# One position's row on TensorE in column groups, single-row products padded to whole blocks, the small products of a Fourier layer placed between its projection blocks

## The chip, the cores and the metric

The kernel runs on one core of a Trainium2 chip. The time is the device time of one execution in microseconds (us), the median of three runs. TensorE (PE, with its weight loads PEld), VectorE (DVE), ScalarE (ACT), GpSimd (POOL) and the queue that issues the DMAs (SP) each work through a list of instructions in order, and semaphores join the lists.

## The reference

One inference step of a two-layer backbone, over 1024 latent positions and 256 context positions of 1024 channels in float32. Layer 0 is attention. Layer 1, where the change lies, mixes by a Fourier transform:

```python
def fourier_mix(u):                      # C_GROUPS = 4, C_GROUP_DIM = 256
    b, s, _ = u.shape
    ug = u.astype(jnp.float32).reshape(b, s, C_GROUPS, C_GROUP_DIM)
    f = jnp.fft.fft2(ug, axes=(1, 3), norm="ortho")
    return jnp.real(f).reshape(b, s, C_WIDTH).astype(u.dtype)

def odd_mix(h, w_in, w_out):
    u, gate = jnp.split(h @ w_in, 2, axis=-1)
    return (fourier_mix(u) * jax.nn.silu(gate)) @ w_out
```

`h` is the normalised and modulated input; the result is scaled, added to the residual and normalised once more. Latent and context positions are transformed apart. The output is y of both, and the keys and values of layer 0.

## The kernel before, in words

Products that need more than one pass of precision are made from three: every operand is split into a high part, rounded to the format that TensorE takes in one pass (fp32r), and the low rest; `mm3` (L244 on, its matmul L250) adds high·high, high·low and low·high in a PSUM bank. A split is a copy on ACT (L262 with ACT, L264 with DVE) and a subtraction on DVE or POOL (L268). SBUF is a set of zones of equal buffers (`u`, `w`, `q`, `pt`, `p`, `h`, `e`); `take` and `drop` hand them round, so a tile is named after its zone. PSUM has eight banks: three `s`, one `a`, one `g`, handed out in turn by `next_bank`, and three `t` for transposes. The Python code is not the order of the instructions: a scheduler with a simulated clock sorts them onto the engines.

The Fourier layer's stages, in the order of the code from L1449 on:

- **The one position.** The transform along the positions uses its symmetry: positions are folded into sums and differences, `EH["E"]`, `EH["O"]` and, for the context, `EH["C"]`. One latent position (column 256 of `O`) and one context position (column 128 of `C`) have no partner. Their rows of the projection are computed by themselves. `xo` holds these two columns of the input. `u_load` (L1473) fetches the weights of a projection step (`load_w`, L274) and calls `row` on each raw weight tile: 128 x 2 x 258, two of eight chunks of the contraction. `row` (L1481, L1483) multiplies each chunk by its `xo` scalar per partition on DVE and adds it up in `xacc`: 8 chunks x 2 positions x 2 weight halves = 32 DVE instructions of 128x258. At the start of step n = 2 `xacc` is split, and eight matmuls with a column of ones (`ux`, L1542) add it up over the partitions. The result stands in one partition, `xrow`, and its split in `xrh`, two tiles of one row.
- **The projection blocks.** Four steps n (cosine weights for n = 0, 1; sine weights for n = 2, 3), five position tiles i each. A block is 24 matmuls of 128x258 (n = 0, 1) or 128x256, into a bank named `u` of `next_bank`. Then ACT copies the bank's halves to the high part (L1581), DVE subtracts for the low part (L1582) and, for n = 0 and 1, copies out the columns at frequency 128, `nyr` (L1584). A bank is free when all of these have read it. The blocks of n = 0 and 1 read `E` and, for i = 4, `C`, the others `O` and `C`.
- **The tables.** Cosine and sine tables (`cosl`, `sinl`, `ctab`) are loaded and split while n = 2 and 3 run (`table`, L1491 on); `oddr` is one row that the one position's row is multiplied with.
- **The small products**, after the last block: `pn` and `pn2` (L1609, L1627), the cosine sum of the columns at frequency 128: 21 matmuls with 4 output rows, three pairs of them with one row of contraction only (the position's row times `oddr`); `p5` (L1631), 16 matmuls with two output rows, and `pcol` (L1654), which turns their result into a column. DVE multiplies by the gates and writes to memory (`nyd`).
- **The transform along the positions**: `pcc` for the context, then per channel group g a bank `pc` and a bank `ps` (all L1609). `pcc` has one pair of single-row matmuls per group, `pc` two. DVE and POOL combine the banks and multiply by the gates (L1669 to L1715).
- **The output projection** `of` (L250 by way of `out_proj`), ten tiles of positions with two banks of 24 matmuls of 128x512.

## Time and profile before

| | us |
|---|---|
| median of three runs | 1232.87 (1231.98 to 1237.57) |
| the profiled execution, its own time | 1240.12 |
| its span on the core | 1238.3 |
| busy in the span: PE / PEld / DVE | 1177.0 / 1048.1 / 868.8 |
| busy in the span: ACT / POOL | 580.4 / 313.9 |
| mean granted TensorE clock | 0.976 |

How the views are read: a row of the timeline has the start of the first instruction, the time from that start to the end of the last of the group, engine, line, operation, result <- operands, `rows*columns` of the weights that a matmul uses, the output's shape, and the count. A matmul lasts some 0.28 us by itself but is pipelined, so what one costs is the step from one start to the next. A row of the stages has the stretch, its length, the busy time of the five engines with the instructions in brackets, the granted TensorE clock (1.00 is full speed), the mean share of the DMA engines and GB/s. In a row of the waits the time comes first after the pair, then how often, then the longest. The order of the instructions has no times in it.

### The profile page before, as it was taken

To read this page: it belongs to the slowest core of one execution; us is meant where nothing else is said; L and a number is where in the kernel's file an instruction comes from. 1 tells how busy PE (TensorE), PEld (TensorE's weight loads), DVE (VectorE), ACT (ScalarE), POOL (GpSimd) and SP (SyncE) were. 2 spreads that over 40 slices of the span, in tenths; PEclk is the share of its full clock that TensorE was granted. 3 is DMA by queue.
4 is the path that set the end of the run, shared out by engine and by line. 5 is a ranking of instruction groups with operands and counts; after the bars stand their busy time and mean duration, and the time that the engine had idled before them with its cause. 6 is when DMAs were issued, how large, how long until landed. Compare 5 with 4: busy or idle time off the path is not lost.

```text
span 1238.3 us, 21899 instructions
## 1 busy us (share of the span) xinstructions
PE 1177.0 (95%) x8039; PEld 1048.1 (85%) x8039; DVE 868.8 (70%) x2023; ACT 580.4 (47%) x1163; POOL 313.9 (25%) x270
## 2 busy tenths in 40 slices
PE   6889999999999999999999989889999998999997
PEld 5778889999999998999999877667778888988886
DVE  4378888877676776678878766667766887558553
ACT  3342456555565555556656766422363234332221
POOL 2264543513221230011000033111312225334001
PEclk9999999999999999999999999979999998979999
DMA  9957312323414252344242695777115434254321
GB/s 334 344 171 264 86 58 75 92 82 109 137 60 125 65 155 67 100 111 129 76 135 84 170 266 169 193 220 215 53 43 161 142 116 127 95 187 154 129 91 63
DMA packets 148686, 168.81 MB, mean 136 GB/s; under 512 B 19753, under 2 KB 107605, under 8 KB 148578
## 3 DMA queue, kind: packets, MB, share of 16 engines
q1 hardware_dynamic: 148578, 167.41, 44.3%
q8 instruction: 63, 1.03, 0.3%
q14 instruction: 45, 0.37, 0.1%
HBM read 123.19 MB, written 44.18 MB: 135 GB/s over the span
## 4 chain that ended last, share of the span: by engine, by line
PE 71%; DMA 13%; DVE 8%; ACT 3%; issue 2%; SPq 1%; POOL 1%; POOLq 0%; DVEq 0%; ACTq 0%
PE of L250 9%; PE ga L250 8%; PE av L1012 7%; PE pt L1006 7%; PE q L250 6%; PE oz L250 6%; PE sL L889 4%; PE g1E L250 4%; PE u L250 3%; PE g1O L250 3%; PE kv L250 2%; PE sC L889 2%; DMA h<-i_w_out 2%; DMA q<-qd 2%; DMA u<-i_x 1%
## 5 line engine op out<-in xcount | busy, mean ns | idle before, releaser
L1009 DVE TENSOR_TENSOR pt<-pt,pt 128x512 fp32r<-128x512 f32 (+1 forms) x264 | 171.2, 658 | 44.8 <-ACT pt L262 44.0
L262 ACT ACTIVATE pt<-pt 128x512 fp32r<-128x512 f32 (+1 forms) x264 | 146.6, 576 | 93.3 <-PE pt L1006 60.7
L1012 PE MATMUL av<-pt,u 128*128 128x256 f32 x1008 | 171.1, 291 | 2.1 <-DVE e L1024 1.0
L1006 PE MATMUL pt<-identr,p 128*128 128x128 f32 x1008 | 155.7, 273 | 3.0 <-ACT e L987 2.5
L1012 PEld LDWEIGHTS av<-pt,u 128*128 128x128 f32 x1008 | 141.5, 191 | 7.9 <-DVE e L1024 2.1
L250 PE MATMUL q<-w,u 128*128 128x256 f32 x864 | 133.0, 289 | 1.5 <-DVE u L426 1.2
L1006 PEld LDWEIGHTS pt<-identr,p 128*128 128x128 f32 x1008 | 119.2, 141 | 9.6 <-ACT e L987 2.7
L250 PE MATMUL ga<-u,w 128*128 128x512 f32 (+1 forms) x576 | 124.2, 359 | 0.0
L250 PEld LDWEIGHTS q<-w,u 128*128 128x128 f32 x864 | 116.2, 191 | 6.4 <-DVE u L426 1.5
L930 ACT ACTIVATE p<-p,nm 128x1280 f32<-128x1280 f32 (+1 forms) x80 | 95.3, 1191 | 55.7 <-DVE p L923 52.5
L250 PEld LDWEIGHTS ga<-u,w 128*128 128x128 f32 x576 | 93.6, 188 | 13.5
L268 POOL TENSOR_TENSOR w<-h,w 128x512 fp32r<-128x512 f32 x42 | 56.7, 1369 | 124.6 <-DVE w L264 88.1
L889 PE MATMUL sL<-u,q 128*128 128x512 f32 x256 | 82.3, 413 | 4.8 <-DMA q<-qd 4.8
L930 ACT ACTIVATE p<-p,NM 128x640 f32<-128x640 f32 (+2 forms) x80 | 59.1, 739 | 25.1 <-DVE p L923 24.8
L268 POOL TENSOR_TENSOR u<-h,u 128x512 fp32r<-128x512 f32 x19 | 25.8, 1359 | 173.6 <-ACT u L262 161.0
L889 PE MATMUL sC<-u,q 128*128 128x256 f32 x320 | 64.9, 303 | 0.6 <-DMA q<-qd 0.6
L250 PE MATMUL oz<-u,u 128*128 128x512 f32 x240 | 62.8, 396 | 2.0 <-ACT h L262 1.1
L923 DVE TENSOR_SCALAR_CACHE_REDUCE p<-sL 128x512 f32<-128x512 f32 x64 | 43.8, 684 | 26.2 <-PE sL L889 13.2
L665 POOL TENSOR_TENSOR h<-h,rope 128x512 f32<-128x512 f32 (+1 forms) x18 | 21.6, 1202 | 139.5 <-ACT h L748 100.1
L250 PE MATMUL kv<-w,u 128*128 128x256 f32 x384 | 55.8, 287 | 0.0
L250 PEld LDWEIGHTS oz<-u,u 128*128 128x128 f32 x240 | 44.5, 188 | 12.9 <-ACT h L262 1.3
L889 PEld LDWEIGHTS sC<-u,q 128*128 128x128 f32 x320 | 50.0, 193 | 4.1 <-issue 0.8
(777 smaller groups left out, 2648.9 us busy)
## 6 DMA issues: line engine op xcount, KB each, us to landing
q<-qd SPq DMA_DIRECT2D x80, 256.0 KB
p<-i_ada_w SPq DMA_DIRECT2D x21, 512.0 KB
h<-i_w_in SPq DMA_DIRECT2D x40, 256.0 KB
h<-i_w_out SPq DMA_DIRECT2D x32, 256.0 KB
pt<-i_ada_w SPq DMA_DIRECT2D x14, 512.0 KB
qd<-q SPq DMA_DIRECT2D x22, 256.0 KB
w<-i_wuT SPq DMA_DIRECT2D x8, 512.0 KB
u<-i_x SPq DMA_DIRECT2D x8, 512.0 KB
```

Source lines behind the costliest of these rows:

```text
L250: pe.matmul(out, a, b, start=i == 0, stop=i == n - 1)
L262: act.activation(out, in_, AF.Copy)
L268: pick("lo" + lc, lc).tensor_sub(dst_l, src, dst_h)
L665: pick("rope", XE["rope"]).tensor_mul(t1.rearrange("p t h (b c) -> p t (h b) c", b=2), y.rearrange("p t h (b c) -> p t (h b) c", b=2), cb)
L889: pe.matmul(ps, q_at(q, s, hc), keys, start=s == 0, stop=s == 1)
L923: dve.tensor_scalar(p[i][:, end[i] : end[i] + n], ps, sign, last[i], op0=ALU.mult, op1=ALU.min, accum_out=c)
L930: act.activation(p[i][:, 0 : end[i]], p[i][:, 0 : end[i]], AF.Exp, bias=last[i], scale=-1.0, accum_out=SU[:, t, hd + i, 0:1],)
L1006: pe.transpose(tp[:, jj * 256 + i * P : jj * 256 + i * P + P], p[i][:, off : off + P], ident)
L1009: dve.tensor_sub(pt[:, 1, 0:n], tp[:, 0:n], pt[:, 0, 0:n])
L1012: pe.matmul(acc, vv, pt[:, s, jj * 256 : jj * 256 + 256], start=c + jj + s == 0, stop=c + jj == nt - 1 and s == 1,)
```

## The change

1. `row` no longer runs on DVE. `xo` is widened to 32 columns per chunk, of which two are not zero, and is the weights of four matmuls per raw tile, each 128 rows deep, with 130 columns moving, into 32 output partitions of a `t` bank `xr0` or `xr1`: two chunks x two halves, so the four stand side by side in the columns of the array. They are plain float32, which the program issues as two passes each. One ACT copy per weight half takes the bank out (`xsum`), and eight small float32 matmuls with a selection matrix (`selx`) add the two chunks up into two partitions (`ux`, `ux2`).
2. `xrh` and `oddr` become tiles of 128 rows of which two are not zero (POOL fills them with zeros first). So the single-row matmuls in `pn`, `pn2`, `pcc` and `pc` run over 128 rows.
3. `pn`, `pn2` and `pcol` are placed after the blocks i = 0, 1 and 2 of n = 3 (`AT_F`), in `t` banks. `p5` is gone: `pcol` now takes sixteen matmuls with the blocks of y as weights and the two columns of `alt` moving.

```diff
+AT_F = (0, 1, 2)
...
-    xo = cp.tile([P, 8, 2], F32, name="xo")
+    xo = take("e", (P, 8, 32))
+    pool.memset(xo.a, 0.0)
...
-    xacc = take(("u", "w", "p"), (P, 2, 516))
+    selx = cp.tile([P, 2, 2], F32, name="selx")
+    iv = ident.rearrange("p (a h c) -> p a h c", a=2, h=2)
+    dve.tensor_add(selx, iv[:, 0, :, 0:2], iv[:, 1, :, 0:2])
+    xsum = [take(("u", "w", "p"), (P, 130)) for _ in range(2)]
...
-    xrh = [take(("u", "w", "p"), (1, 2, 516), F32R) for _ in range(2)]
+    xrh = [take(("u", "w", "p"), (P, 516), F32R) for _ in range(2)]
...
     def u_load(n):
         c, hf = divmod(n, 2)
+        ps = t_bank(f"xr{hf}") if c == 0 else None
+
         def row(raw, k0):
-            for v in range(2):
-                acc = xacc[:, v, hf * 258 : hf * 258 + 258]
-                for k in (k0, k0 + 1):
-                    x = raw[:, k - k0, :]
-                    if k == 0:
-                        dve.tensor_scalar(acc, x, xo[:, k, v : v + 1], None, op0=ALU.mult)
-                    else:
-                        dve.scalar_tensor_tensor(
-                            out=acc, in0=x, scalar=xo[:, k, v : v + 1], in1=acc, op0=ALU.mult, op1=ALU.add
-                        )
+            for kk in range(2):
+                for h in range(2):
+                    j = 2 * kk + h
+                    pe.matmul(
+                        ps[32 * j : 32 * j + 32, 0:130], xo[:, k0 + kk, :], raw[:, kk, 128 * h : 128 * h + 130],
+                        start=k0 == 0, stop=k0 == 6,
+                    )
+            if k0 == 6:
+                act.activation(xsum[hf].a, ps[:, 0:130], AF.Copy)
...
+    def fine_part(i):
+        if i == 0:
+            fine["a"] = t_bank("pn")
+            cos_pair(fine["a"][0:4, :], ny, xn(0))
+        elif i == 1:
+            fine["b"] = t_bank("pn2")
+            cos_sum(fine["b"][0:4, 0:256], [ny(4)], [ctcol(0)], xn(1), oddr[:, 512:768])
...
+        elif i == 2:
+            pcol = t_bank("pcol")
+            for g in range(4):
+                for n in range(4):
+                    pe.matmul(pcol[:, 2 * g : 2 * g + 2], y_at(0, n // 2, g)[n % 2], alt, start=n == 0, stop=n == 3)
+            dve.tensor_scalar(p5c, pcol[:, 0:8:2], scale, None, op0=ALU.mult)
...
-            xh, xl = [take(("u", "w", "p"), (P, 2, 516), F32R) for _ in range(2)]
-            act.activation(xh.a, xacc.a, AF.Copy)
-            dve.tensor_sub(xl.a, xacc.a, xh.a)
...
-                    ps = next_bank(f"ux{h2}{v}")[0:2, 0:258]
-                    for m, x in enumerate((xh, xl)):
-                        pe.matmul(ps, ones2[:, 0, :], x[:, v, sl], start=m == 0, stop=m == 1)
...
+                    out = ps[0:2, (2 * h2 + h) * P : (2 * h2 + h) * P + P]
+                    pe.matmul(out, selx[:, h, :], xsum[h2][:, h : h + P], start=True, stop=True)
...
+            for x in xrh:
+                pool.memset(x.a.bitcast(F32), 0.0)
...
-            oddr, oraw = take(BIG, (1, 768), F32R), take(BIG, (1, 768))
+            oddr, oraw = take(BIG, (P, 768), F32R), take(BIG, (2, 768))
+            pool.memset(oddr.a.bitcast(F32), 0.0)
...
+            if n == 3 and i in AT_F:
+                fine_part(AT_F.index(i))
...
-    cos_pair(pn[0:4, :], ny, xn(0))
...
-            pe.matmul(p5[0:2, g * P : g * P + P], alt, y_at(0, n // 2, g)[n % 2], start=n == 0, stop=n == 3)
```

What the scheduler makes of it is shown at three places, as the rows of the order stand, before and after. **DVE, where the first projection blocks are taken out of PSUM.** L1483 and L1481 are the position's row, L1582 and L1584 (after: L1674 and L1676) the evacuation of a bank `u`, L1394 (L1395) a gate. Before:

```order
L1483 SCALAR_TENSOR_TENSOR p_12065<-w_12110,xo,p_12065 128x258 x2
L1483 SCALAR_TENSOR_TENSOR p_12065<-p_12118,xo,p_12065 128x258 x4
L1483 SCALAR_TENSOR_TENSOR p_12065<-pt_12128,xo,p_12065 128x258 x2
L1582 TENSOR_TENSOR u_12169<-u_12176,u_12169 128x128
L1483 SCALAR_TENSOR_TENSOR p_12065<-pt_12128,xo,p_12065 128x258 x2
L1582 TENSOR_TENSOR u_12169<-u_12206,u_12169 128x128
L1483 SCALAR_TENSOR_TENSOR p_12065<-q_12136,xo,p_12065 128x258
L1582 TENSOR_TENSOR u_12172<-u_12176,u_12172 128x128
L1584 COPY nyr<-u_12176 128x2
```

After:

```order
L1434 TENSOR_TENSOR h_12021<-g1c_11994,h_12019 128x128
L1395 SCALAR_TENSOR_TENSOR h_12021<-u_12024,h_12021 128x256
L1674 TENSOR_TENSOR u_12177<-u_12184,u_12177 128x128
L1674 TENSOR_TENSOR u_12180<-u_12184,u_12180 128x128
L1676 COPY nyr<-u_12184 128x2
L1674 TENSOR_TENSOR u_12177<-u_12214,u_12177 128x128
```

The evacuation of the first bank now follows the last gate directly.

**PE, at the start of the projection.** `ad12p` is a small sum of another row, `xr` the new matmuls in column groups. Before:

```order
L353 MATMUL ad12p_12029<-h_12036,ones_88 2x512
L250 MATMUL u_12176<-w_12072,w_10787 128x258
L250 MATMUL u_12176<-p_12073,w_10787 128x258
L250 MATMUL u_12176<-w_12072,w_10788 128x258
L250 MATMUL u_12176<-w_12072,p_10811 128x258
```

After:

```order
L354 MATMUL ad12p_12029<-h_12036,ones_88 2x512
L1487 MATMUL xr_12076<-pt_12079,e_12058 32x130 x4
L1487 MATMUL xr_12076<-q_12087,e_12058 32x130
L354 MATMUL ad12p_12029<-h_12037,ones_88 2x512
L1487 MATMUL xr_12076<-pt_12097,e_12058 32x130 x4
L251 MATMUL u_12184<-p_12077,w_10787 128x258
L251 MATMUL u_12184<-u_12078,w_10787 128x258
L1487 MATMUL xr_12076<-w_12105,e_12058 32x130 x4
L251 MATMUL u_12184<-p_12077,w_10788 128x258
```

The 32 matmuls of `xr` stand in six sets, of 5, 7, 4, 4, 4 and 8, within and between the first blocks; a set reads the raw weight tile straight from its DMA.

**SP, around the loads of the tables.** `i_cosl` is the cosine table, `i_w_out` weights of the output projection into buffers `h`, `g1d` gates. Before:

```order
L1068 DMA h_12939<-i_w_out 128x512
L1068 DMA h_12925<-i_w_out 128x512
L1567 DMA h_12706<-g1d 4x256
L1564 DMA p_12703<-g1d 128x4x256
L1498 DMA u_12690<-i_sinl 128x1024
L1498 DMA u_12531<-i_cosl 128x1024
```

After:

```order
L1069 DMA h_12942<-i_w_out 128x512
L1069 DMA h_12922<-i_w_out 128x512
L1069 DMA h_12926<-i_w_out 128x512
L1069 DMA h_12932<-i_w_out 128x512
L1069 DMA h_12936<-i_w_out 128x512
L1505 DMA u_12695<-i_sinl 128x1024
L1647 DMA w_12700<-i_oddr 2x768
L1656 DMA u_12707<-g1d 128x4x256
L1656 DMA w_12709<-g1d 128x4x256
L1505 DMA u_12536<-i_cosl 128x1024
```

Five loads of output weights instead of two now stand ahead of the tables, and both gate loads ahead of the cosine table, which `pn` reads after sixteen blocks instead of twenty. The last four of the five use buffers `h` that held the raw sine weights of n = 3.

## The prediction

> **What bounds the kernel now.** I read the page first, then the stages of the Fourier layer, then PE's timeline inside them. TensorE is busy almost throughout, so a gain must come from PE's own time:

> ```profile
> PE 1177.0 (95%) x8039; PEld 1048.1 (85%) x8039; DVE 868.8 (70%) x2023; ACT 580.4 (47%) x1163; POOL 313.9 (25%) x270
> ```

> The stages tell where that time is poor. Columns: stretch, length, busy PE, PEld, DVE, ACT, POOL, granted TensorE clock, DMA share, GB/s.

> ```profile
> 1033.30:1037.40 4.10, 0.14 (x2) 0.07 (x1) 4.10 (x13) 2.27 (x6) 1.52 (x4) 0.88 0.47 126
> 1036.00:1037.00 1.00, 0.00 (x0) 0.00 (x0) 1.00 (x3) 0.74 (x3) 0.31 (x2) 0.71 0.03 8
> 1043.00:1044.00 1.00, 1.00 (x9) 1.00 (x8) 0.17 (x2) 0.00 (x0) 1.00 (x2) 0.88 0.61 205
> 1094.00:1095.00 1.00, 1.00 (x6) 0.64 (x5) 0.96 (x2) 0.00 (x0) 0.93 (x1) 0.72 0.50 174
> 1108.00:1109.00 1.00, 1.00 (x10) 1.00 (x10) 0.87 (x2) 0.09 (x1) 0.00 (x0) 0.95 0.12 49
> ```

> PE stands still from 1033.3 to 1037.4 while DVE is busy for all of it. The clock is 1.00 or 0.50: a mean of 0.71 in 1036 to 1037 puts the fall at 1036.42, 0.88 puts the return at 1043.24, and in the same way the second stretch at half speed runs from 1094.44 to 1108.10. These stretches are 6.82 and 13.66 us long, and the falls lie 58.02 apart: 2, 4 and 17 times 3.41, as if the clock were set anew every 3.41 us on a grid of its own. What ended the standstill, and DVE's work there:

> ```profile
> 1037.36 1.63 PE L250 MATMUL u<-u,w 128*128 128x258 f32 x6 [3.96 <-DVE nyr L1584]
> L1483 DVE SCALAR_TENSOR_TENSOR p<-w,xo,p 128x258 f32<-128x258 f32 x6 | 5.8, 999 | 0.0
> L1481 DVE TENSOR_SCALAR p<-w,xo 128x258 f32<-128x258 f32 x2 | 2.7, 1391 | 0.0
> ```

> PE waited for a bank, whose last reader on DVE (L1584) stood behind the position's row; two groups of that row alone cost 8.5 us.

> **The change part by part.** The stretch in question goes from the end of the gates to the first `of`. Single costs come from these rows (start, length, count):

> ```profile
> 1019.84 0.86 PE L353 MATMUL ad12p<-h,ones 128*2 128x512 f32 x3
> 1050.27 4.37 PE L250 MATMUL u<-u,u 128*128 128x258 f32 x35
> 1087.11 0.86 PE L1609 MATMUL pn<-u,nyq 128*4 128x256 f32 x6
> 1087.90 0.39 PE L1609 MATMUL pn<-w,nyq 1*4 1x256 f32 x2
> 1088.22 0.86 PE L1609 MATMUL pn<-u,nyq 128*4 128x256 f32 x6
> 1090.22 0.64 PE L1631 MATMUL p<-u,alt 128*2 128x128 f32 x8
> 1090.70 0.64 PE L1631 MATMUL p<-w,alt 128*2 128x128 f32 x8
> 1091.18 0.57 PE L1609 MATMUL pcc<-h,u 128*128 128x256 f32 x3
> 1092.65 1.05 PE L1654 MATMUL pcol<-identr,h 1*128 1x2 f32 x8
> 1093.63 0.62 PE L1609 MATMUL pcc<-h,u 128*128 128x256 f32 x3
> 1109.05 0.86 PE L1609 MATMUL pc<-u,u 128*128 128x256 f32 x6
> 1109.84 0.50 PE L1609 MATMUL pc<-w,u 1*128 1x256 f32 x2
> 1110.27 0.97 PE L1609 MATMUL pc<-u,u 128*128 128x256 f32 x6
> 1111.59 0.38 PE L1609 MATMUL ps<-p,p 128*128 128x256 f32 x1
> 1119.88 0.86 PE L250 MATMUL of<-u,w 128*128 128x512 f32 x3
> ```

> The stretch is 1019.84 to 1119.88, 100.0 us. A plain matmul of 258 columns steps by (4.37 - 0.28) / 34 = 0.12, one of 256 (as in `pn`) by (0.86 - 0.28) / 5 = 0.116.

> *a, the standstill.* The 32 DVE instructions go, so L1584 follows at once: +4.0. Next to come late would be the bank's ACT copy behind the last weight splits; five banks cover some 14 us of PE work (5 x 24 x 0.12), so I count nothing for it.

> *b, the half clock behind it.* From 1037.36 to 1043.24 PE worked at half speed for 5.9 us: +2.9 if PE no longer idles.

> *c, the second half-clock stretch.* 13.7 us at half speed: +6.8 if the clock does not fall there. The 3.41 us before 1094.44 held pairs with one row (`pcc`) and `pcol`, and no idle time; the 3.41 us before that, with `pn`, four columns wide but 128 rows deep, had not lowered the clock. So what counts seems to be rows that move, not columns, and the padding restores them; I expect no fall in their place. [...]

> *d, single rows.* At full clock one `pc` took 1111.59 - 1109.05 = 2.54 for 16, against 16 x 0.116 = 1.86: 0.34 for each of its two pairs. `pcc` and `pc` have twelve pairs: +4.1. *e:* in `pn` a group of eight took 1.11 (1087.11 to 1088.22), against 0.93: 0.18 a pair, three pairs, +0.5. Ends of d and e together: 15 pairs at 0.18 and at 0.34, 2.7 to 5.1.

> *f, the new sets.* The form is in the trace of before, in the modulation of layer 0, with 128 columns instead of 130:

> ```profile
> 80.42 0.64 PE L464 MATMUL ad<-p,e 128*32 128x128 f32 x16
> 80.89 0.62 PE L464 MATMUL ad<-pt,e 128*32 128x128 f32 x16
> 103.93 0.60 PE L250 MATMUL q<-w,u 128*128 128x256 f32 x3
> 104.45 0.64 PE L464 MATMUL ad<-p,e 128*32 128x128 f32 x16
> 105.03 0.50 PE L250 MATMUL q<-w,u 128*128 128x256 f32 x2
> 80.00:121.00 41.00, 38.30 (x582) 33.98 (x586) 31.22 (x88) 10.10 (x24) 18.73 (x21) 1.00 0.81 278
> ```

> In a run sixteen passes take 0.47, 0.029 each. Coming from full matmuls the first starts 0.17 late (103.93 + 3 x 0.12 = 104.28), and the next full one comes 0.58 after it, 0.11 more than steady: 0.28 a visit. 64 passes and six visits: 1.9 + 1.7 = -3.6; ends -1.9 (no visit cost) and -4.2 (eight visits). The clock stayed 1.00 through 41 us of this mixture. The sets also make PE wait for the raw tiles' DMAs themselves, with every later block behind:

> ```profile
> 1018.49 0.99 SPq L283 DMA_DIRECT2D w<-wcd  x2
> 1021.35 0.64 ACT L262 ACTIVATE u<-w 128x516 fp32r<-128x516 f32 x1 [1.03 <-DMA w<-wcd]
> ```

> From issue to first use a tile took 2.9. The last two reuse buffers that PE's own first sets free at about 1021, so they are there by some 1025 to 1026; ahead of them PE has seven `ad12p` (0.24 each), 48 passes in five visits (2.8) and 30 block matmuls (3.6), and comes to them at 1027.9. I count no wait; each microsecond that they are later costs one. [...]

> *g, `ux`.* Eight matmuls (1.0) become eight passes of 128 columns in one column group (8 x 4 x 0.029 = 0.9) and eight of two columns, which I price like the smallest step above, 0.06: -0.4. Between zero and -0.9.

> *h, `p5` and `pcol`.* 0.96 (1090.22 to 1091.18) and 0.98 (1092.65 to 1093.63) become sixteen loads of whole blocks with two columns moving. The nearest row with such loads is a transpose:

> ```profile
> 70.83 1.04 PE L401 MATMUL xt<-identr,u 128*128 128x128 f32 x8
> ```

> (1.04 - 0.28) / 7 = 0.11 each, 1.75: +0.2; at 0.06 each +1.0, at 0.12 nothing.

> *i, the end.* The evacuation on DVE after the first `ps` to the last split of the output weights, and PE's first use of it:

> ```profile
> 1108.13 0.69 DVE L1703 TENSOR_TENSOR u<-pc,h 128x512 f32<-128x512 f32 x1 [4.63 <-ACT h L1701]
> 1134.31 0.68 DVE L268 TENSOR_TENSOR w<-h,p 128x512 fp32r<-128x512 f32 x1
> 1135.42 0.40 PE L250 MATMUL of<-w,w 128*128 128x512 f32 x1
> ```

> DVE needs 26.9 us there and its work is the same after the change. PE took 27.3 and saves 0.68 in each of three `pc`: it would be there 1.6 before the split. I count -2.0; ends 0 and -5.

> Hidden, at no cost: the POOL fills, POOL being busy 25%, and the DVE products behind `pn2`, which go between evacuations; the product of `p5c` with a gate tile now stands ahead of the last evacuations on DVE and waits for that tile's load, which SP issues once PE has read the first part of `O` for the last time. If one of these runs late, PE has the banks' 14 us before it waits; beyond that it costs what it is late.

> Sum: 4.0 + 2.9 + 6.8 + 4.1 + 0.5 - 3.6 - 0.4 + 0.2 - 2.0 = 12.5 against the profiled execution: its own 1240.12 (the span of 1238.3 and 1.8 around it) becomes 1227.6. That execution lies 7.3 above the median of the runs shown. If the clock's grid runs free of the program, a standstill of 4.0 will not always fill 3.41 of it: I take half of b for the median, 11.0 in all, and forecast 1232.87 - 11.0 = **1221.9**.

> **The rivals.**

> *The clock falls again.* If what counted before 1094.44 was `pcol`, in which next to nothing moves, the new `pcol` does the same for 1.75 of 3.41 us. For it: the clock fell with no idle time in the rows. Against: transposes load whole blocks likewise, and blocks now lie around it, so it should end after 3.41. Price 1.7 for one step of the grid to 6.8 for four: up to 1228.7. [...] Chance 0.13.

> *The tables come late, and the change is slower.* `pn` stands in PE's list after block 16 and waits for the split cosine table.

> ```profile
> 1058.13 0.33 SPq L1498 DMA_DIRECT2D u<-i_cosl  x1
> 1056.93 2.54 POOL L268 TENSOR_TENSOR u<-h,u 128x512 fp32r<-128x512 f32 x2 [12.27 <-PE u L250]
> 1064.56 2.66 POOL L268 TENSOR_TENSOR u<-u,u 128x1024 fp32r<-128x1024 f32 x1
> SPq L1068 <- DVE u L268: 11.4, 1, 11.4
> ```

> From issue to split it took 9.1 (1058.13 to 1067.22). PE reaches `pn` at about 1087.11 - 4 x 24 x 0.116 - 2.9 = 1073.1 (four blocks earlier, and 2.9 gained ahead of it by a, b, f and g). POOL's splits of the sine weights are released by PE at 1056.93 - 3.3 = 1053.6 (a, b and f); four at 1.27 end at 1058.7, three loads more at some 0.5 put the issue at 1060.2, the split at 1069.3, and 1.3 MB more ahead of it at the 278 GB/s of the row above add up to 4.7: 1069.3 to 1074.0. So PE waits 0 to 0.9, for which I count nothing; a mild delay of up to 5 us gives 1222 to 1227, around 1225, chance 0.08. If SP is held at one of these loads as it once was, for 11.4 (last row), the split comes at 1080.7 to 1085.4 and PE waits 8 to 12, with a half-clock stretch behind it that loses 2.9 to 6.8, as the two measured ones do. Each microsecond after 1073.1 costs one; with the longer stretch the gain of 11.0 is gone from 1077 on, and at 1085.4 the time is 1221.9 + 12.3 + 6.8 = 1241.0. Against it: that wait fell on a load behind all tables, and the sine splits are due in time. Chance 0.06.

> **How the numbers follow.** Forecast 0.73, clock 0.13, mild delay 0.08, slower 0.06. The good ends of b, d, e, f and i, with the rest as taken (4.0 + 2.9 + 6.8 + 5.1 - 1.9 - 0.4 + 0.2), give 16.7 less: low 1216.2. The clock's fall at its worst gives 1228.7: high 1229.0. The slow case stays outside, and a little beyond either end. About 0.5%, 6.2 us, is what a measurement of this kernel can tell from no change, so faster means below 1226.7: the forecast nearly whole (0.70), a third of the clock's case (0.04), most of the mild delay (0.06): 0.80. Within: 0.14. Slower: 0.06.

> **What would show it.** Right: no wait of PE on L1676 after 1033, clock 1.00 from there to `of`, steps of 0.12 in all of `pcc` and `pc`, the `xr` sets at 3 to 4 us, the stretch from `ad12p` to `of` at 86 us instead of 100. Wrong: PE waiting at `pn` for POOL or a DMA, 0.50 in the clock column behind `pcol`, or the first `of` early and PE then waiting for the last output weights by as much. If the stretch shrinks by 14 and the span by less than 9, term i was too small.

## The result and the profile after

The changed kernel took 1223.73 us (median of 6 runs, 1221.91 to 1225.89), the kernel before beside it 1234.59 (1230.38 to 1237.57): a ratio of 0.991, 95% interval 0.9884 to 0.9936, 10.9 us less; 1221.9 was forecast, 11.0 less. Measured again later (experiment 5) the same kernel came to 0.9957 (0.9934 to 0.9979), 1230.98 beside 1235.73, 4.8 us less. The two intervals barely touch. A part of the gain comes and goes from one execution to the next, which turned out to be the main finding of this study; but it does not explain why the two measurements differ (experiment 5).

The profiled execution of the changed kernel took 1225.89, its span is 1224.1 instead of 1238.3. Of the 14.2, 3.7 lie ahead of the change: the first `ad12p` starts at 1016.16 instead of 1019.84, and in the other profiles of both kernels it starts anywhere from 1014.8 to 1021.4. So below every kernel is judged by the time from its first `ad12p` to the end of its span: 218.5 before, 207.9 after, 10.5 less.

The page's line of PE, and then the stages of the Fourier layer in the changed kernel:

```profile
PE 1164.8 (95%) x8103; PEld 1038.7 (85%) x8103; DVE 841.6 (69%) x1990; ACT 580.1 (47%) x1163; POOL 314.9 (26%) x274
```

```profile
1016.00:1102.00 86.00, 84.55 (x742) 80.06 (x741) 37.22 (x97) 34.62 (x86) 40.37 (x37) 1.00 0.50 160
1086.60:1101.76 15.16, 15.16 (x131) 15.16 (x130) 12.45 (x19) 8.11 (x17) 9.59 (x7) 1.00 0.77 265
```

The granted clock is 1.00 over the whole 86 us; both half-clock stretches of the kernel before are gone. PE's timeline, at the places of the prediction's terms:

```profile
1016.16 0.86 PE L354 MATMUL ad12p<-h,ones 128*2 128x512 f32 x3
...
1018.64 0.28 PE L251 MATMUL u<-u,w 128*128 128x258 f32 x1
1018.85 0.43 PE L1487 MATMUL xr<-w,e 128*32 128x130 f32 x8
1019.20 0.51 PE L251 MATMUL u<-p,w 128*128 128x258 f32 x2
1019.55 0.28 PE L251 MATMUL u<-u,w 128*128 128x258 f32 x1
...
1038.86 0.36 PE L251 MATMUL u<-p,u 128*128 128x258 f32 x1 [1.45 <-DVE nyr L1676]
...
1052.48 0.60 PE L1616 MATMUL ux<-p,selx 128*2 128x128 f32 x4
...
1053.63 0.73 PE L251 MATMUL u<-u,u 128*128 128x256 f32 x4
...
1070.81 1.81 PE L1550 MATMUL pn<-u,nyq 128*4 128x256 f32 x14
...
1072.69 0.28 PE L251 MATMUL u<-q,u 128*128 128x256 f32 x1
...
1079.13 0.95 PE L1598 MATMUL pcol<-alt,u 128*128 128x2 f32 x8
...
1080.83 0.37 PE L251 MATMUL u<-q,u 128*128 128x256 f32 x1
...
1091.35 1.93 PE L1550 MATMUL pc<-u,u 128*128 128x256 f32 x15
1093.12 0.28 PE L1550 MATMUL pc<-u,w 128*128 128x256 f32 x1
1093.24 0.39 PE L1550 MATMUL ps<-w,u 128*128 128x256 f32 x2
...
1101.76 0.40 PE L251 MATMUL of<-u,u 128*128 128x512 f32 x1
...
1105.70 1.82 PE L1550 MATMUL pc<-u,p 128*128 128x256 f32 x14
...
1108.06 0.50 PE L251 MATMUL of<-u,u 128*128 128x512 f32 x1 [0.30 <-DVE u L1729]
...
1121.18 0.51 PE L251 MATMUL of<-w,u 128*128 128x512 f32 x1 [0.93 <-DVE w L269]
```

Three things are to be seen. One `pc` takes 1093.24 - 1091.35 = 1.89 instead of 2.54. PE still stands still once, for 1.45 at 1037.4, again for `nyr` on DVE. And in the output projection, where PE had not waited at all in the profile before, it waits twice for DVE. The stretch from `ad12p` to the first `of` is 85.6, but the last `pc` (1108.06 - 0.30 - 1105.70 = 2.1) now stands behind the first `of`: like for like it is 87.7, 12.4 less than the 100.04 before; the rest of the kernel takes 120.3 instead of 118.4, 1.9 more.

The standstill at 1037.4 in the timeline of SP's queue and of DVE:

```profile
1034.01 0.36 SPq L1505 DMA_DIRECT2D h<-i_ctab  x1
...
1038.02 0.43 DVE L265 CAST h<-h 128x512 fp32r<-128x512 f32 x1 [3.80 <-DMA h<-i_ctab]
1038.36 0.28 DVE L1674 TENSOR_TENSOR u<-u,u 128x128 fp32r<-128x128 f32 x1
1038.56 0.15 DVE L1676 COPY nyr<-u 128x2 f32<-128x2 f32 x1
```

DVE itself has nothing to do, but in its list the split of the context table (`ctab`, L265) stands ahead of the evacuations, and it waits 3.80 for a load that was issued only at 1034.01. With the position's row gone from DVE, the scheduler had put this split there.

### The profile page after: what moved, and what is told of

It is laid out like the page before. It is cut to its first block, busy times and chain, and to the rows that moved or that the text cites. A ratio compares the mean times of both kernels' runs of the same rounds, so it can differ in the third digit from the quotient of the medians.

```text
span 1224.1 us, 21997 instructions
## 1 busy us (share of the span) xinstructions
PE 1164.8 (95%) x8103; PEld 1038.7 (85%) x8103; DVE 841.6 (69%) x1990; ACT 580.1 (47%) x1163; POOL 314.9 (26%) x274
## 3 DMA queue, kind: packets, MB, share of 16 engines
q8 instruction: 64, 1.05, 0.4%
```

## Theories

- **A**, the prediction's: rows that move keep the clock up; the single rows lowered it before 1094, always; the position's row on DVE caused the standstill; what PE saves beyond a point is given back at the end, where DVE is late (term i).
- **B**: `pn` and `pcol`, with few columns, lowered the clock.
- **C**: the gain comes from where the small products stand.
- **A2**, formed after experiments 1 to 4: the clock goes down after a step of 3.41 us (the unit of the two stretches before, 6.82 and 13.66) in which PE moves too few columns through whole blocks, whatever takes the time; the grid of steps runs free of the program, so the same program may or may not be hit.

## The experiments

**1. Padding alone** (`pad_only`), in the kernel before:

```diff
-    xrh = [take(("u", "w", "p"), (1, 2, 516), F32R) for _ in range(2)]
+    xrh = [take(("u", "w", "p"), (P, 2, 516), F32R) for _ in range(2)]
...
+            for x in xrh:
+                pool.memset(x.a.bitcast(F32), 0.0)
+            dve.tensor_copy(xrh[0][0:1, :, :], xrow.a)
...
+            oddr, oraw = take(BIG, (P, 768), F32R), take(BIG, (1, 768))
+            pool.memset(oddr.a.bitcast(F32), 0.0)
...
-        cos_sum(out[:, 0:256], [y(0), y(1)], [tcol(tcos, 0), tcol(tcos, 1)], [v[0:1] for v in y(2)], oddr[:, 0:256])
+        cos_sum(out[:, 0:256], [y(0), y(1)], [tcol(tcos, 0), tcol(tcos, 1)], y(2), oddr[:, 0:256])
...
```

> The kernel before with only the single rows padded to 128 rows; the position's row stays on DVE, pn, pn2, p5 and pcol stay where they were. Theory A (terms c, d, e of the prediction: too few rows moving lowered the clock before 1094): no second half-clock stretch and fifteen pairs cheaper, 6.8 + 4.6 = 11 us less than before, ratio 0.991; the standstill of 4 us near 1033 and the half clock behind it stay. Theory B (pcol or pn, with few columns, lowered the clock): only the pairs get cheaper, 4.6 us less, ratio 0.996, and half clock stays behind pcol. Theory C (placing carries the gain): no change.

Measured: 0.9942 (0.9915 to 0.9969), between the two figures. The stage around `pcol`, and PE's waits in its timeline:

```profile
1087.00:1110.00 23.00, 23.00 (x199) 22.00 (x197) 18.97 (x36) 11.18 (x23) 14.54 (x11) 1.00 0.72 241
```

```profile
1038.33 1.36 PE L250 MATMUL u<-u,w 128*128 128x258 f32 x6 [4.01 <-DVE nyr L1587]
1115.33 0.94 PE L250 MATMUL of<-u,w 128*128 128x512 f32 x3 [0.97 <-DVE u L1707]
1121.67 0.50 PE L250 MATMUL of<-u,w 128*128 128x512 f32 x1 [1.44 <-DVE u L268]
1127.78 0.50 PE L250 MATMUL of<-w,w 128*128 128x512 f32 x1 [0.75 <-DVE w L268]
```

The clock stays at 1.00 behind `pcol`, although `pcol` and `p5` are as they were. That speaks against B, but it is one profile, and the unaltered kernel can do the same (experiments 8 to 10); the count of columns behind them decides it. The standstill of 4.0 stays, as expected. From `ad12p` to the end it takes 210.0. And 3.2 of what PE saves comes back at once as three waits for DVE in the output projection: term i, here larger than in the changed kernel.

**2. The row back on DVE** (`row_on_dve`), in the changed kernel: `row`, `xacc` and the eight `ux` matmuls as before the change, the row's two positions side by side in one partition of padded tiles.

```diff
-                    pe.matmul(
-                        ps[32 * j : 32 * j + 32, 0:130], xo[:, k0 + kk, :], raw[:, kk, 128 * h : 128 * h + 130],
...
+                        dve.scalar_tensor_tensor(
+                            out=acc, in0=x, scalar=xo[:, k, v : v + 1], in1=acc, op0=ALU.mult, op1=ALU.add
+                        )
```

> The changed kernel with the position's row back on DVE; padding and placing stay. Theory A (terms a, b, f, g): the standstill of 4 us near the start of the blocks and half clock behind it come back, the sets of xr go: 4.0 + 2.9 - 3.6 - 0.4 = 2.9 slower than the changed kernel, about 1226.6; since the changed kernel still stands still for 1.5 there, rather 1.4 slower, 1225. Rival (the row on DVE is hidden): 4 us faster than the changed kernel, as the xr sets are pure cost.

Measured: 0.9918 (0.9886 to 0.995); from `ad12p` to the end 208.7, 0.8 more than the changed kernel. PE's standstill in its timeline, and the stage around it:

```profile
1034.75 1.63 PE L251 MATMUL u<-u,w 128*128 128x258 f32 x6 [4.16 <-DVE nyr L1660]
```

```profile
1033.00:1039.00 6.00, 4.25 (x20) 4.28 (x21) 4.49 (x13) 2.81 (x8) 3.86 (x3) 0.50 0.26 90
```

Standstill and half clock are back as forecast, the sets of `xr` are gone, and the two nearly cancel: by the profiles, computing the row on PE is worth 0.3 to 0.8 us (208.7 against 208.4 and 207.9), not the four that its standstill cost, and the runs don't tell the two kernels apart.

**3. The small products last** (`small_last`), in the changed kernel:

```diff
-            if n == 3 and i in AT_F:
-                fine_part(AT_F.index(i))
         drop_w(w)
+    for i in range(3):
+        fine_part(i)
```

> The changed kernel with pn, pn2 and the new pcol after the last projection block, next to each other, as before the change. Theory A (rows that move keep the clock): the same time as the changed kernel within 1.5 us and clock 1.00. Theory B (pcol with two moving columns and pn with four output rows lower the clock): half clock behind pcol, 1.7 to 6.8 us slower. Theory C (placing matters since the evacuation of pn and its writes to memory need the time): PE waits for nyd or for banks, 2 us or more slower with clock 1.00.

Measured: 0.9903 (0.9871 to 0.9936), 208.4 from `ad12p` to the end, 0.5 more than the changed kernel. The clock in the step of the grid that holds all of `pcol` and the end of `pn`, and in the next:

```profile
1087.07:1090.48 3.41, 3.41 (x34) 3.12 (x33) 2.73 (x10) 0.00 (x0) 0.15 (x1) 1.00 0.13 48
1090.48:1093.89 3.41, 3.41 (x31) 3.41 (x30) 1.82 (x6) 0.77 (x2) 1.40 (x2) 1.00 0.57 152
```

No half clock, and no gain from the placing that could be measured: against C, and in this one profile against B.

**4. Padded tiles, of which two rows are read** (`two_rows`), in the changed kernel:

```diff
-        return [xrh[i][:, g * 129 : g * 129 + P] for i in range(2)]
+        return [xrh[i][0:2, g * 129 : g * 129 + P] for i in range(2)]
...
-        cos_sum(pcc[:, 0:256], [y_at(0, 4, g)], [ctcol(0)], xg(1, g), oddr[:, 512:768])
+        cos_sum(pcc[:, 0:256], [y_at(0, 4, g)], [ctcol(0)], xg(1, g), oddr[0:2, 512:768])
```

> The changed kernel with the padded tiles, of which the matmuls read only the first two rows. Theory A: the pairs cost 0.34 again (12 of them, 4.1 us, and 0.5 in pn), and the clock falls to one half behind pcc for 6.8 to 13.7 us, which costs 3.4 to 6.8 more: 8 to 11.4 slower, 1232 to 1235. Theory B: the pairs cost 4.6, the clock stays 1.00: 1228. [...]

Measured: 0.9954 (0.9931 to 0.9976), 210.6 from `ad12p` to the end, 2.7 more than the changed kernel. `pcc` in PE's timeline, and the stage:

```profile
1089.52 0.52 PE L1550 MATMUL pcc<-h,u 128*128 128x256 f32 x3
1089.97 0.38 PE L1550 MATMUL pcc<-u,u 2*128 2x256 f32 x1
...
1094.85 0.28 PE L1550 MATMUL ps<-w,u 128*128 128x256 f32 x1
```

```profile
1089.00:1108.00 19.00, 19.00 (x130) 16.31 (x130) 14.68 (x23) 9.12 (x19) 9.52 (x7) 1.00 0.74 255
```

The four `pcc` take 1094.85 - 1089.52 = 5.33 instead of 1090.41 - 1086.60 = 3.81 in the changed kernel: 0.38 a pair, so term d has its price. But the clock stays at 1.00. In this profile few rows alone don't lower it, against theory A, as experiment 1 was against B. What is left is the sum of both: in the kernel before, the 3.41 us ahead of the fall held pairs with one row *and* `pcol`. This is A2, and the next runs test it.

**5. The changed kernel again** (`after_again`).

> The changed kernel itself, unaltered, on the same chip as the next three. By every theory: 0.991 of the kernel before, the interval of its first runs; clock 1.00 from the start of the blocks to the output projection, and a standstill of PE of about 1.5 behind the split of the context table on DVE.

Measured: 0.9957 (0.9934 to 0.9979), less gain than expected; but its own profile says the same as the first one: clock 1.00, standstill 1.52, waits of 0.36 and 1.24 at the end, 208.4 from `ad12p` to the end.

```profile
1018.90:1104.60 85.70, 84.18 (x740) 79.78 (x738) 36.16 (x95) 33.92 (x84) 40.28 (x37) 1.00 0.51 160
```

The kernel before hardly moved between the two measurements (1234.59 and 1235.73); the changed kernel did (1223.73 and 1230.98), and of these 7.3 us its two profiles show 0.5 behind `ad12p` and 2.7 ahead of the change. So, as far as two profiles can tell, most of the difference doesn't come from the stretch that the change touches, and its cause stays open.

The runs of the kernel before gave another hint. Of the 35 beside this one, 14 took 1229.07 to 1232.39 and 21 took 1234.58 to 1242.74, none between, as if something came and went. Elsewhere the two groups are not to be seen: the 20 runs beside experiments 1 to 4 lie between 1230.68 and 1247.66 without such a gap. So the hint had to be followed in profiles (experiments 8 to 10).

**6. Two rows and the small products last** (`two_rows_last`): the edits of 3 and 4 together.

> The changed kernel with the matmuls of the padded tiles reading two rows only and with pn, pn2 and pcol after the last projection block. Neither alone made the clock fall. Theory A2 (dead time of single-row pairs and of pcol adds up in a step of 3.41): here they stand side by side, the step holds 0.31 to 0.48 of the possible columns, the clock falls to one half behind pcol for 6.8 to 13.7 us, 3.4 to 6.8 slower than with two rows alone. Theory A1 (single rows in one row, not two, are what counts): clock 1.00 and the time of two rows alone. Theory B (the fall in the kernel before is chance): no relation.

Measured: 1.0022 (0.9999 to 1.0045); 215.8 from `ad12p` to the end, 5.2 more than with two rows alone. The stages, at the step with the rest of `pcol` and behind it:

```profile
1088.51:1091.92 3.41, 3.41 (x27) 3.01 (x26) 1.92 (x9) 0.38 (x1) 0.00 (x0) 1.00 0.14 43
1092.00:1105.00 13.00, 13.00 (x50) 10.98 (x49) 4.92 (x10) 3.33 (x7) 6.34 (x5) 0.50 0.56 190
1105.00:1106.00 1.00, 1.00 (x8) 1.00 (x8) 0.34 (x1) 0.97 (x2) 0.00 (x0) 0.71 0.00 0
```

Neither edit alone lowered the clock; together they do, at 1091.92, for 13.7 us, as long as in the kernel before. PE is busy in every row.

**7. `pcol` three times in a row** (`pcol_thrice`), in the changed kernel; the added matmuls write the same values again.

```diff
-            for g in range(4):
+            for g in (0, 1, 2, 3) * 3:
```

> The changed kernel with the sixteen matmuls of pcol run three times in a row (the later ones overwrite the same bank), so that for 5.4 us, more than one step of 3.41, whole blocks are loaded and two columns move. Added work: 32 x 0.11 = 3.5 us. Theory A as the prediction put it (rows that move decide, whole blocks keep the clock): clock stays 1.00, 3.5 slower than the changed kernel. Theory A2 (what decides is how many columns move in a step of the grid: 0.39 of the possible ones in the step before the fall of the kernel before, 0.69 or more elsewhere): the clock falls to one half for at least 3.41 behind it, 1.7 to 3.4 more, 5.2 to 7 slower.

Measured: 0.9989 (0.9963 to 1.0014); 214.4 from `ad12p` to the end, 6.0 to 6.4 more than the changed kernel's two profiles, as A2 has it.

```profile
1078.47:1081.88 3.41, 3.41 (x33) 3.41 (x32) 0.89 (x2) 1.43 (x3) 1.39 (x2) 1.00 0.20 73
1082.00:1088.00 6.00, 6.00 (x29) 6.00 (x30) 0.16 (x1) 0.00 (x0) 0.22 (x1) 0.50 0.21 66
1088.00:1089.00 1.00, 1.00 (x8) 1.00 (x8) 0.00 (x0) 0.00 (x0) 0.00 (x0) 0.65 0.34 131
```

PE and its weight loads are busy for all of the step, whole blocks are loaded, two columns of each move: the clock falls.

**8 to 10. The kernel before, profiled three more times** (`before_a`, `before_b`, `before_c`).

> The kernel before, unaltered, profiled again (three times, this is the first). Its times fall into a group near 1231.5 with clocks around 0.985 and a spread above 1234.5 with clocks around 0.980, some 60 per cent of them. Theory A2 (the clock is set on a grid of 3.41 us that runs free of the program; whether a step holds too few columns depends on where the grid lies): of three profiles one or two show no half clock behind pcol, and there the step that covers pcol also holds blocks or the full part of pn, so that it holds 0.5 of the possible columns or more; these end some 7 us earlier after ad12p (211 to 212, not 218.5). Theory A as the prediction took it (always): half clock of 13.7 us behind pcol in all three.

> As the run before: the kernel before, second profile. Theory A2: half clock behind pcol in about 0.6 of the profiles; theory A: in each.

> As the two runs before: the kernel before, third profile. Theory A2: half clock behind pcol in about 0.6 of the profiles; theory A: in each.

Measured: `before_a` and `before_b` keep the clock at 1.00 behind `pcol` and take 211.6 and 211.9 from `ad12p` to the end; `before_c` falls for 10.2 us and takes 213.8. Their own times don't tell which is which: `before_b` without the fall took 1233.24, `before_c` with it 1233.15, as the part ahead of `ad12p` differs by 2.0. Of `before_a` the step with `pcol`, then of `before_c` the step ahead of the fall and the fall:

```profile
1087.60:1091.01 3.41, 3.41 (x32) 3.00 (x30) 2.27 (x9) 0.97 (x2) 0.00 (x0) 1.00 0.16 48
1091.01:1094.43 3.42, 3.42 (x22) 2.61 (x21) 1.54 (x4) 0.90 (x2) 2.31 (x2) 1.00 0.65 199
```

```profile
1087.31:1090.72 3.41, 3.41 (x23) 2.86 (x23) 2.22 (x5) 1.15 (x3) 1.34 (x2) 1.00 0.64 207
1091.00:1100.00 9.00, 9.00 (x35) 7.66 (x35) 3.37 (x8) 1.80 (x4) 5.04 (x4) 0.50 0.58 165
```

The order of the instructions is the same; only the grid lies elsewhere. In the clock's record of `before` and of `after` each change from 1.00 to 0.50 or back lies a whole number of steps of 3.41 behind the last one: 1 to 158 steps in `before`, 1 to 194 in `after`. I laid the grid of each profile through its own changes of clock, and counted from PE's timeline the columns that matmuls with 128 rows move in a step (256 for each matmul of `pcc`, 2 for one of `pcol`, none for a pair with one or two rows; a step of plain blocks holds 3.41 / 0.118 x 256 = 7400, with 0.118 from the 1.89 of the 16 matmuls of one `pc`):

| profile | step | columns | clock behind it |
|---|---|---|---|
| `pcol_thrice` | 1078.47 to 1081.88 | 60 | 0.50 |
| `two_rows_last` | 1088.51 to 1091.92 | 2300 | 0.50 |
| before | 1091.03 to 1094.44 | 2600 | 0.50 |
| `before_c` | 1087.31 to 1090.72 | 2900 | 0.50 |
| `small_last` | 1087.07 to 1090.48 | 3200 | 1.00 |
| `before_a` | 1087.60 to 1091.01 | 3400 | 1.00 |
| `before_b` | 1088.80 to 1092.21 | 3400 | 1.00 |
| `two_rows`, its poorest | 1089.77 to 1093.18 | 3600 | 1.00 |
| `pad_only`, its poorest | 1089.86 to 1093.27 | 4700 | 1.00 |

The count also serves where there is only one profile. A window of 3.41 us that is slid along PE's timeline from 1060 to 1112 finds 3360 columns at its poorest place in both profiles of the changed kernel (at the standstill that is left, 3354 at the least), 4360 in `pad_only`, 3328 in `two_rows` and 3112 in `small_last`. So, as an estimate from these counts, no position of the grid would lower the clock there, in `small_last` only just. In `before_a` and `before_b` the poorest place holds 2048, and the poor windows start within a stretch of 2.2 us, so that a grid of 3.41 should meet one in about two of three executions (an estimate, 2.2 / 3.41); two of four profiles fell. In `two_rows_last` the poorest place holds 1064, in `pcol_thrice` 42, and in `ctab_pool` of experiment 11, around a wait of 2.28, 1792.

The border is a count over the products of this layer. Early in the kernel it fails: in `two_rows` the step at 76.00 holds twelve transposes of 128 columns, 1536 in all, PE is busy for 2.05 of 3.41, and the clock stays at 1.00 behind it. What the clock goes by in general is not shown here.

```profile
76.00:79.41 3.41, 2.05 (x12) 1.30 (x12) 2.95 (x5) 3.38 (x8) 3.41 (x4) 1.00 0.00 0
79.42:82.82 3.40, 2.83 (x49) 2.56 (x53) 3.33 (x10) 2.68 (x6) 0.23 (x1) 1.00 0.00 0
```

**11. The context table split on POOL** (`ctab_pool`), in the changed kernel:

```diff
-            split(h.a, l.a, raw.a, "ad", "pd")
+            split(h.a, l.a, raw.a, *(("p", "p") if m <= 512 else ("a", "p")))
```

> The changed kernel with the context table split on POOL alone, so that DVE's evacuations no longer queue behind its load. Theory A (the 1.45 us of standstill left in the changed kernel come from DVE's wait for that load): no wait of PE on L1676, 1.5 us faster than the changed kernel; of it up to 1.5 may come back at the end, where DVE's evacuation is late already (there PE waits 1.2 in the changed kernel, and would wait up to 2.7): between 1.5 faster and no change. Rival (the bank is held by something else): the wait stays.

Measured: 0.9946 (0.9923 to 0.997), 208.2 from `ad12p` to the end, no less than the changed kernel (207.9 and 208.4). The stage with the former standstill, and PE's waits in its timeline:

```profile
1030.00:1040.00 10.00, 10.00 (x85) 10.00 (x85) 2.45 (x12) 4.89 (x14) 5.91 (x9) 1.00 0.40 108
```

```profile
1109.33 0.47 PE L251 MATMUL of<-u,u 128*128 128x512 f32 x1 [2.28 <-DVE u L1729]
1122.44 0.50 PE L251 MATMUL of<-w,u 128*128 128x512 f32 x1 [1.28 <-DVE w L269]
```

The edit also keeps the two larger tables off DVE, but in the changed kernel's profile they were split on ACT and POOL anyway. The standstill is gone, so the context table was its cause; and the 1.5 us come back as longer waits at the end, 3.6 instead of 1.2 and 1.6. That points to DVE's end as the bound from here on, which experiment 12 tests.

**12. DVE relieved at its end** (`light_tail`), in addition to 11:

```diff
-        dve.tensor_copy(ds[:, :, 512:513], ds[:, :, 256:257])
+        act.activation(ds[:, :, 512:513], ds[:, :, 256:257], AF.Copy)
...
-        dve.tensor_scalar(M[g // 2][2][:, cc, 0:1], gt[1][:, :, 0:1], p5c[:, g : g + 1], None, op0=ALU.mult)
+        act.activation(M[g // 2][2][:, cc, 0:1], gt[1][:, :, 0:1], AF.Copy, scale=p5c[:, g : g + 1])
```

> The changed kernel with the context table split on POOL and, besides, with DVE's small copies and its products of p5c with a gate column (two lines behind the evacuation of pc) moved to ACT, which is idle for half of that time. Theory T (DVE, busy without a break from the first pc to the last split of the output weights, sets the end; term i): 3 us less on DVE, so PE's waits of 2.3 and 1.3 on DVE in the output projection shrink to 0.5 to 1.5 together, from the first ad12p to the end 205 to 206.5 instead of 208.2. Rival (the gate tile's load sets the last of these waits): the wait for the last output weights stays at 1.3, and DVE waits for the load instead; 207.

Measured: 0.9887 (0.9843 to 0.9931), 1225.12 beside 1236.18; 205.7 from `ad12p` to the end, 2.2 to 2.7 less than the changed kernel and the shortest of all. What PE still waits for:

```profile
1111.98 0.47 PE L251 MATMUL of<-u,u 128*128 128x512 f32 x1 [1.16 <-DVE u L1729]
```

Of 3.6 us of waits 1.2 are left: DVE's end was the bound, as term i had it, and the wait for the last output weights is gone, against the rival. By its profile this version is ahead of both kernels; by the runs it is ahead of the kernel before, but its interval overlaps that of the changed kernel's first measurement, so the runs don't show it ahead of the changed kernel.

## Why the prediction was right, and where it was wrong

The forecast of 11.0 less met the first measurement (10.9) and is more than twice the second (4.8). By the profiles, the four of the kernel before take 218.5, 211.6, 211.9 and 213.8 from `ad12p` to the end, 214.0 in the mean, and the two of the changed kernel 207.9 and 208.4, 208.2 in the mean: 5.8 less. So the hit on the first measurement is in part luck: most terms were right, but the two largest that failed, a and c, were too big for the mean of the profiles.

- **a, the standstill (+4.0; measured +2.5).** The row's 32 instructions did hold L1584 up (experiment 2 brings 4.16 back), but 1.45 stayed, and in `before_c` the standstill was only 3.20. I looked at ACT for what would be late next; it was DVE again, whose list had a table's split moved into the gap. "No wait of PE on L1676 after 1033" was the sign I named, and it failed.
- **b, the half clock behind it (+2.9 in the profile, half of it for the median).** No half clock is left in the profile. In the four profiles of the kernel before PE worked at half speed there for 5.9, 3.4, 3.4 and 0 us after it resumed: a mean cost of 1.6, so the half was right; that the grid runs free, on which it rested, was then a guess from one profile.
- **c, the second half-clock stretch (+6.8, taken as certain).** This is the term that was mis-sized, and with a wrong reason. It cost 6.8 in the profile that I had, 5.1 in another and nothing in two: 3.0 in the mean. I gave b a share because the grid runs free and did not ask the same of c. The reason, rows that move and not columns, fell in both halves: two rows alone keep the clock (4: 1.00 from 1089 to 1108), and whole blocks with two columns lose it (7: 0.50 from 1082 on). The grid did not follow the program: in the four profiles of the kernel before the fall lies 3.3 us behind the start of `pcc` (1094.44), 5.2 behind it (1090.72), or is missing twice. Nor does a fall need an idle PE: in runs 6 and 7 half clock followed steps in which the profile shows PE busy for 3.41 of 3.41.
- **d and e, the pairs (+4.1 and +0.5).** Right: 0.65 for each `pc` (1.89 instead of 2.54), 0.38 for each pair in `pcc` by experiment 4 (with two rows), 1.5 + 4 x 0.65 = 4.1; the first sixteen matmuls of `pn` took 1072.69 - 1070.81 = 1.88, instead of 2 x 1.11.
- **f, the `xr` sets (-3.6).** Right: a set of four (eight passes) puts 1019.20 - 1018.64 = 0.56 between two matmuls that are otherwise 0.12 apart, and 0.11 behind the next; the six sets, worked out likewise, come to 3.9. No set waited for its DMA.
- **g, h (-0.4, +0.2).** `ux` took 1.15 instead of 1.0, `pcol` 1080.83 - 1079.13 = 1.70 and 0.08 behind it, instead of 1.94 for `p5` and `pcol`: -0.2 and +0.2.
- **i, the end (-2.0).** Right in size (1.9) and in kind, and it turned out to be the bound of the new kernel: experiment 1 pays 3.2 there, experiment 11 gives its whole gain back there, experiment 12 gains there. This is also why the parts of the change don't add up: without a fall of the clock, padding alone gains 211.8 - 210.0 = 1.8, and everything together 3.6, while PE's own work shrinks by more.
- **The rivals.** The clock did not fall in the changed kernel's two profiles; that `pcol` can do it is shown by experiment 7, where it ran for more than a step of 3.41; its 1.7 us among full blocks left 3360 columns in the poorest window. The tables were not late at `pn`: the cosine table's load was issued at 1052.59, not at 1060.2, and its split ended ten microseconds before PE came. A table did make PE wait, but another one, at another place, through DVE's list.

In the first profile the terms as measured, 2.5 + 2.9 + 6.8 + 4.1 + 0.5 - 3.9 - 0.2 + 0.2 - 1.9 = 11.0, stand against 10.5; half a microsecond is not accounted for. With the means of all profiles for a (3.8 before, 1.5 after: 2.3), b (1.6) and c (3.0) they come to 5.7, against 5.8.

## What to carry to other kernels

A stretch at half clock that the profile of one execution shows may be missing from the next (the second stretch of the kernel before stood in two of four profiles): profile the kernel several times before its whole length is put into a sum. In this layer a product of which little moved (two columns, or one row between whole blocks) cost its own step (0.11 each in the new `pcol`, 0.34 more for a pair of single rows in `pc`) and, where enough of them filled a step of the clock's grid (the 20 steps of 3.41 us ahead of half clock held 3072 columns or fewer), the clock besides; so look how many full products stand around it. With the rows padded, spreading the small products among full blocks gained no time that could be measured (0.5 us in experiment 3), it only left more room to the border (3360 columns in the poorest window instead of 3112). And when work is taken off an engine that works through a list, look at what the scheduler puts into the gap and at the next place where that engine ends last; here both took part of the gain (1.45 and 1.9).

## What was not expected of the hardware

- The clock fell with PE and its weight loads busy for 3.41 of 3.41 in the step ahead (experiment 7, 1078.47 to 1081.88), and in the stretches behind `pcol` it came back after two, three or four steps of 3.41 (6.8, 10.2 and 13.7 us).
- Two rows cost as much as one: a pair between whole blocks took 0.33 to 0.38 us more than its two plain steps of 0.12, a pair padded with zeros to 128 rows no more than these (a `pc` of 16 took 1.89 in the changed kernel, 0.118 each).
- A product of 128x2 elements on DVE took 0.21 or 1.16; beside the second POOL worked from 1120.34 to 1122.04, beside the first it did not. On ACT it took 0.30. These are rows of `after_again` (DVE) and of `light_tail` (ACT):

```profile
1107.22 0.21 DVE L1740 TENSOR_SCALAR u<-u,p5c 128x2 f32<-128x2 f32 x1
1120.91 1.16 DVE L1740 TENSOR_SCALAR u<-u,p5c 128x2 f32<-128x2 f32 x1
```

```profile
1121.32 0.30 ACT L1740 ACTIVATE u<-u,p5c 128x2 f32<-128x2 f32 x1 [4.02 <-DMA u<-g1d]
```
